# The first FFN matrix of a transformer step as 2x2 blocks in seven products, in six phases

## The chip, the cores and the metric

The kernel runs on one core of one Trainium2 chip. Times are microseconds (us) on the device for one execution. TensorE (PE in the profile, its weight loads PEld) does the matrix products, VectorE (DVE) and ScalarE (ACT) the elementwise work, GpSimd (POOL) masks and small copies, SyncE (SP) issues the DMAs.

## What is computed

One layer of a streaming encoder for 512 prompt rows and 8 x 16 sample rows, 640 rows of 1024 values in all: three token mixers with gates, cross-attention, and a SwiGLU FFN with 2816 hidden channels, each between two RMS norms with a residual. The change concerns the FFN:

```python
def swiglu(h, w_in, w_out):
    g, u = jnp.split(h @ w_in, 2, axis=-1)
    return (jax.nn.silu(g) * u) @ w_out
...
    h = rmsnorm(x, p['norm_ffn_pre'][l])
    x = x + rmsnorm(swiglu(h, p['w_ffn_in'][l], p['w_ffn_out'][l]), p['norm_ffn_post'][l]).astype(x.dtype)
```

All inputs and outputs are 32-bit floats.

## The kernel before

Every large matrix product is made from two parts of each operand: `split` (L141) writes the leading bits of a tile as a cast on ACT and what is left as a subtraction on DVE, and three matmuls (leading x leading, and the two mixed ones) are accumulated for each block of 128 rows of the contraction. Weights arrive by DMA in `raw` tiles (three buffers, L67) and are split into `wh` and `wl` (four buffers each) by `split_w`.

The last stage before the FFN is the output projection of the cross-attention, `ProjD` (L856). Its `finish` (L877) goes over the five tiles of 128 rows: the products of the second column half, the norm, the addition to the residual `X` in SBUF, and the norm ahead of the FFN (`normed`, L187). Two tiles behind, `after_xo` (L1122) transposes the normed rows on TensorE and splits them into `fT_h` and `fT_l` (8 blocks of 128 channels by 640 rows). The calls for the last two tiles are returned as `behind` and come inside the FFN.

The FFN runs in two phases (`ffn_phase`, L1136) of eleven channel units. A unit (`ffn_unit`, L1147) is 128 gate and 128 up channels: 24 matmuls into bank `pg`, Silu on ACT, 24 into `pu`, the product on DVE, and the split into `ga_h`, `ga_l`; once for rows 0 to 383 and once for rows 384 to 639 (`PARTS`). Its weights are two `raw` tiles, each from two DMAs of 256 KB. Then the second matrix follows for the eleven channel tiles, in two column halves (L1177): five accumulators of 128 rows by 512 columns, 3 matmuls for each channel tile and accumulator (L1199 to L1201). `finish` (L1208) evicts an accumulator: in phase 0 by a copy on ACT into `Y`, in phase 1 by an addition to `Y` on DVE, the gain, and a sum of squares on ACT. In the last column half each tile of rows is then normed, added to `X` and stored.

The framework puts the instructions of each engine into one fixed order, by the order of the program and by when their operands are ready in its own model, and adds the waits. Each engine takes its instructions in that order. A tile with n buffers makes a new writer wait for the readers of the n-th last one. PSUM has eight banks, two for each of the tags `g`, `t`, `z` and `o`. Silu and the pair Ln and Exp (`rstd_of`, L146) need different tables on ACT, and a change of table is a load.

## Time and profile before

| | |
|---|---|
| median of three runs | 1338.93 us (1330.9, 1338.93, 1339.3) |
| the profiled execution: its time | not listed by itself among the three; 1330.9 is below its span |
| the profiled execution: its span, first to last instruction | 1332.9 us |
| instructions | 21503 |
| mean granted TensorE clock | 0.995 of full speed |
| DMA | 128.65 MB, 97 GB/s over the span |

The profile is of one execution. A busy time counts an engine's instructions. A matmul row lasts from the start of its weights' use to the modelled end of its last column, so neighbouring rows overlap: the pace is the distance of their starts. In the chain of waits one row is a stretch of instructions on one engine, each followed back to what released it.

### The profile page before, as it was taken

The page shows a single profiled execution, that of the slowest core. Times are in us where ns is not written, and L with a number is a line of the kernel's source. Part 1 is how long each engine was busy: PE and PEld are TensorE (multiplying, and loading weights), DVE is VectorE, ACT ScalarE, POOL GpSimd, SP SyncE. Part 2 cuts the span into 40 slices and gives each one's busy share as a digit, 9 for nine tenths or more (in the row PEclk, how much of TensorE's full clock was granted, in tenths as well). Part 3 has the DMA queues.
Part 4 walks back from the last instruction along what each step waited for, and adds up shares of the span by engine and source line. Part 5 has one row for each costly group of instructions (what it writes and reads, how often), then busy time and mean ns, then how long its engine had stood idle before and what let it go on. Part 6 is the DMA issues. An engine that isn't in the chain of part 4 may idle for free.

```text
span 1332.9 us, 21503 instructions
## 1 busy us (share of the span) xinstructions
PE 1313.9 (99%) x8754; PEld 1194.7 (90%) x8754; DVE 629.3 (47%) x1242; ACT 541.5 (41%) x1087; POOL 41.3 (3%) x162
## 2 busy tenths in 40 slices
PE   9999999999999999999999999999999999999997
PEld 8998678988999999979988878899999889999986
DVE  6434775485587454547444434742322112322235
ACT  5324665454353454435444523642222222322222
POOL 2001111001000000000000000000000000000000
PEclk9999999999999999999999999999999999999999
DMA  7324231202412222422368821232222223232212
GB/s 233 112 77 128 82 97 49 60 1 66 116 30 68 84 88 75 144 94 95 127 227 296 270 79 33 70 105 64 84 75 72 72 73 86 64 95 64 75 52 79
DMA packets 134296, 128.65 MB, mean 97 GB/s; under 512 B 15670, under 2 KB 116613, under 8 KB 134197
## 3 DMA queue, kind: packets, MB, share of 16 engines
q1 hardware_dynamic: 133909, 126.98, 30.7%
q8 instruction: 69, 1.13, 0.3%
q0 software_dynamic: 288, 0.29, 0.1%
q14 instruction: 30, 0.25, 0.1%
HBM read 119.10 MB, written 8.15 MB: 95 GB/s over the span
## 4 chain that ended last, share of the span: by engine, by line
PE 93%; DVE 3%; DMA 2%; ACT 1%; issue 0%; SPq 0%; POOL 0%; DVEq 0%; ACTq 0%
PE ps_g L114 12%; PE pu L114 12%; PE pg L114 12%; PE ps_d L114 8%; PE ps_n L114 7%; PE ps_xq L114 4%; PE ps_b L114 4%; PE acc L1201 4%; PE acc L1199 4%; PE acc L1200 4%; PE ps_qk L114 3%; PE pl L718 2%; PE ps_xk L114 2%; PE ps_xv L114 1%; PE z L505 1%; PE xo L1074 1%
## 5 line engine op out<-in xcount | busy, mean ns | idle before, releaser
L1157 DVE TENSOR_TENSOR s<-pu,s 128x384 f32<-128x384 f32 (+1 forms) x44 | 21.5, 488 | 125.2 <-PE pu L114 125.2
L1199 PE MATMUL acc<-wh_o,ga_h 128*128 128x512 f32 (+1 forms) x168 | 64.5, 384 | 0.0
L1201 PE MATMUL acc<-wh_o,ga_l 128*128 128x512 f32 (+1 forms) x168 | 64.4, 384 | 0.0
L1200 PE MATMUL acc<-wl_o,ga_h 128*128 128x512 f32 (+1 forms) x168 | 64.3, 382 | 0.0
L89 DVE TENSOR_TENSOR wl_o<-raw_o,wh_o 128x1024 fp32r<-128x1024 f32 (+1 forms) x24 | 27.2, 1135 | 77.7 <-ACT wh_o L83 77.5
L1154 ACT ACTIVATE s<-pg 128x384 f32<-128x384 f32 (+1 forms) x44 | 19.3, 439 | 89.6 <-PE pg L114 89.6
L813 ACT ACTIVATE sgm<-ps_g 128x320 f32<-128x320 f32 x48 | 21.0, 437 | 66.0 <-PE ps_g L114 65.9
L83 ACT CAST wh_o<-raw_o 128x1024 fp32r<-128x1024 f32 (+1 forms) x24 | 23.5, 978 | 49.8 <-PE acc L1201 36.7
L143 ACT CAST ga_h<-s 128x384 fp32r<-128x384 f32 (+1 forms) x32 | 14.7, 459 | 63.2 <-DVE s L1157 63.2
L1201 PEld LDWEIGHTS acc<-wh_o,ga_l 128*128 128x128 f32 x168 | 31.5, 188 | 6.8
L1200 PEld LDWEIGHTS acc<-wl_o,ga_h 128*128 128x128 f32 x168 | 31.6, 188 | 6.7
L1199 PEld LDWEIGHTS acc<-wh_o,ga_h 128*128 128x128 f32 x168 | 31.5, 188 | 6.5
L718 PEld LDWEIGHTS pl<-X 96*120 96x120 f32 (+6 forms) x256 | 28.9, 181 | 6.4 <-issue 3.7
L814 DVE TENSOR_SCALAR sgm<-sgm 128x320 f32<-128x320 f32 x48 | 15.5, 325 | 40.4 <-ACT sgm L813 40.3
L718 PE MATMUL pl<-X 96*120 96x64 f32 (+6 forms) x256 | 30.5, 263 | 2.8 <-DVE X L714 2.7
L114 PE MATMUL ps_d<-wh_xo,oT_h 128*128 128x512 f32 x80 | 32.4, 405 | 0.0
L114 PE MATMUL ps_d<-wh_mix,mT_h 128*128 128x512 f32 x80 | 31.9, 398 | 0.0
L114 PE MATMUL ps_d<-wl_xo,oT_h 128*128 128x512 f32 x80 | 31.7, 396 | 0.0
L114 PE MATMUL ps_d<-wh_xo,oT_l 128*128 128x512 f32 x80 | 31.6, 396 | 0.0
L114 PE MATMUL ps_d<-wl_mix,mT_h 128*128 128x512 f32 x80 | 31.6, 395 | 0.0
L114 PE MATMUL ps_d<-wh_mix,mT_l 128*128 128x512 f32 x80 | 31.4, 392 | 0.0
L815 ACT ACTIVATE sgm<-sgm 128x320 f32<-128x320 f32 x48 | 22.5, 469 | 15.8 <-DVE sgm L814 15.7
(1207 smaller groups left out, 4442.1 us busy)
## 6 DMA issues: line engine op xcount, KB each, us to landing
raw_o<-in_w_ffn_out_dram SPq DMA_DIRECT2D x20, 512.0 KB, 3.8
kc<-in_cache_mem_k_dram SPq DMA_DIRECT2D x16, 512.0 KB, 4.8
vc<-in_cache_mem_v_dram SPq DMA_DIRECT2D x16, 512.0 KB, 5.4
raw_mix<-in_w_mix_out_dram SPq DMA_DIRECT2D x8, 512.0 KB, 4.2
raw_xo<-in_w_xo_dram SPq DMA_DIRECT2D x8, 512.0 KB, 6.2
kn<-in_cache_sb_k_dram SPq DMA_DIRECT2D x24, 128.0 KB, 2.5
vn<-in_cache_sb_v_dram SPq DMA_DIRECT2D x24, 128.0 KB, 2.7
out_dram<-X SPq DMA_DIRECT2D x10, 256.0 KB, 2.0
```

The source lines that it names most:

```text
L83: nc.scalar.copy(wh, raw)
L89: (eng or nc.vector).tensor_tensor(wl, raw, wh.bitcast(F32), ALU.subtract)
L114: ins = nc.tensor.matmul(ps, a, b, start=(j == 0), stop=(j == len(todo) - 1))
L718: nc.tensor.matmul(pl[0:nk, h], X[:, h, 0:nk], mv_, start=True, stop=True)
L813: nc.scalar.activation(s, ps, AF.Exp, scale=-1.0)
L814: nc.vector.tensor_scalar(s, s, 2.0 ** 63, None, ALU.min)
L815: nc.scalar.activation(s, s, AF.Ln, bias=1.0)
L1154: nc.scalar.activation(s, pg, AF.Silu)
L1157: nc.vector.tensor_tensor(s, pu, s, ALU.mult)
L1199: nc.tensor.matmul(ps, ah, wh[:, kk, lo:hi], start=(first and kk == 0), stop=False)
L1200: nc.tensor.matmul(ps, ah, wl[:, kk, lo:hi], start=False, stop=False)
L1201: nc.tensor.matmul(ps, al, wh[:, kk, lo:hi], start=False, stop=(last and kk == nk - 1))
```

## The change

Let the 1024 input channels be two halves, the 640 rows two halves of 320, and the gate and up channels of a unit the two column halves. The product of these 2x2 blocks is made from seven block products P1 to P7 (Winograd's form of Strassen's method) in place of eight, for 20 of the 22 units. Each is 4 blocks of 128 channels x 3 matmuls of 320 columns. The right-hand sides are sums of weight blocks (`sums`, four operations on DVE for each unit), the left-hand sides sums of row blocks (`s_prep`, once, on the transposed rows that `after_xo` also copies into `X`), and each is split into two parts. The products share banks: some accumulate onto a bank after ACT or DVE has read it.

The columns of `fT` are put in another order (`cols`): a half of the sample rows and two prompt tiles make 320. The two first units stay plain, with the Silu behind the last Exp and four different banks, and run beside the last two tiles of rows. Six phases of 4, 3, 3, 4, 4 and 4 units follow each other, each with its part of the second matrix; the order of TensorE is written out by hand there (`manual_schedule`). Every phase adds its accumulators to `Y`, which now lies in the memory of `X`; the residual is written to DRAM (`xd`) and read back in the last phase. There all of a tile's columns are finished before the next tile. A weight tile of the second matrix holds one channel tile and all 1024 columns, before two channel tiles and 512 columns. `ProjD.finish` takes the tiles in the order 4, 0, 1, 2, 3, puts the sum into its `Y` and the normed rows into `X`. The rest of the diff takes comments out.

New lines, and context, without the lines that are taken out (those of `ffn_phase`, printed above):

```diff
-        def finish(self, wpool, gain2, done):
+        def finish(self, wpool, gain2, done, order=tuple(range(NT)), in_y=False):
             self.ws = load_w512(self.w2d, 512, 512, self.name + "1")
+            res = self.Y if in_y else X
...
+                    nc.vector.scalar_tensor_tensor(res[:, i, cs], self.Y[:, i, cs], r, X[:, i, cs], ALU.mult, ALU.add)
+                xns[i] = normed(wpool, res[:, i, :], gain2, 3, X[:, i, :] if in_y else None)
...
+    xd = tc.dram_tile([NT, P, D], F32, name="xd")
...
     def after_xo(i, xn):
+        for b, tp in enumerate(transposed(xn)):
+            ks = slice(4 * b, 4 * b + 4)
+            nc.scalar.copy(x32(i)[:, ks, :], tp)
+            src = tp.rearrange("p k (two c) -> p k two c", two=2) if i == 4 else tp
+            split(cols(fT_h[:, ks], i), cols(fT_l[:, ks], i), src)
+    behind = xo.finish(None, g2, after_xo, (4, 0, 1, 2, 3), True)
+    for i in (4, 0, 1, 2, 3):
+        nc.sync.dma_start(xd[i], Y[:, i, :])
...
+    Y = X
+    fw = open_pool("fw", "right")
+    g_post = gain_tile(fw, norm_ffn_post, "gpost")
+    ga_h = fw.tile([P, 4, TOK], F32R, name="ga_h")
+    ga_l = fw.tile([P, 4, TOK], F32R, name="ga_l")
...
+    S_h = hpool.tile([P, 16, H2], F32R, tag="th", name="S_h")
+    S_l = hpool.tile([P, 16, H2], F32R, tag="tl", name="S_l")
+    sub, addop = ALU.subtract, ALU.add
+    def s_prep(a, b, o):
+        w = a.shape[-1]
+        nc.vector.tensor_tensor(b[:, 4:8], b[:, 0:4], b[:, 4:8], addop)
+        nc.vector.tensor_tensor(b[:, 0:4], a[:, 0:4], b[:, 0:4], sub)
+        nc.vector.tensor_tensor(a[:, 0:4], b[:, 4:8], a[:, 0:4], sub)
+        nc.vector.tensor_tensor(a[:, 4:8], a[:, 4:8], a[:, 0:4], sub)
+        split(S_h[:, 0:8, o:o + w], S_l[:, 0:8, o:o + w], b)
+        split(S_h[:, 8:16, o:o + w], S_l[:, 8:16, o:o + w], a)
...
+    def g_split(k, s):
+        (ph_, sh_), (pl_, sl_) = gt(k)
+        two = lambda t: t.rearrange("p (t c) -> p t c", t=2)
+        split(two(ph_), two(pl_), s[:, :, 64:H2])
+        split(two(sh_), two(sl_), s[:, :, 0:64])
...
+    AH = {"P1": ((fT_h, fT_l), 0, 0), "P2": ((fT_h, fT_l), 4, 0), "P4": ((fT_h, fT_l), 4, H2),
+          "P7": ((S_h, S_l), 0, 0), "P5": ((S_h, S_l), 4, 0), "P6": ((S_h, S_l), 8, 0), "P3": ((S_h, S_l), 12, 0)}
...
+        def load(self):
+            wv = w1.rearrange("(k p) c -> p k c", p=P)
+            c0 = self.n * P
+            self.ra = ring.tile([P, 2, 4, P], F32, tag="raw", bufs=3, name="ra")
+            self.rb = ring.tile([P, 2, 4, P], F32, tag="raw", bufs=3, name="rb")
+            for j in range(2):
+                nc.sync.dma_start(self.ra[:, j], wv[:, 0:4, c0 + j * FF:c0 + j * FF + P])
+            for j in range(2):
+                nc.sync.dma_start(self.rb[:, j], wv[:, 4:8, c0 + (1 - j) * FF:c0 + (1 - j) * FF + P])
+        def sums(self):
+            self.ta = fpool.tile([P, 2, 4, P], F32, tag="ta", bufs=1, name="ta")
+            self.t4 = fpool.tile([P, 1, 4, P], F32, tag="t4", bufs=1, name="t4")
+            ra, rb, ta = self.ra, self.rb, self.ta
+            nc.vector.tensor_tensor(ta[:, 1], rb[:, 0], ra[:, 1], sub)
+            nc.vector.tensor_tensor(ta[:, 0], ra[:, 1], ra[:, 0], sub)
+            nc.vector.tensor_tensor(ra[:, 1], ta[:, 1], ra[:, 0], addop)
+            nc.vector.tensor_tensor(self.t4[:, 0], rb[:, 1], ra[:, 1], sub)
+        def parts(self, which):
+            src, names = {"ra": (self.ra, ("P1", "P6")), "ta": (self.ta, ("P5", "P7")),
+                          "rb": (self.rb, ("P3", "P2")), "t4": (self.t4, ("P4",))}[which]
+            pool, tags, bufs = (fpool, ("t4h", "t4l"), 1) if which == "t4" else (ring, ("wh", "wl"), 4)
+            h = pool.tile(list(src.shape), F32R, tag=tags[0], bufs=bufs, name="wh_f")
+            l = pool.tile(list(src.shape), F32R, tag=tags[1], bufs=bufs, name="wl_f")
+            split(h, l, src)
+            for j, nm in enumerate(names):
+                self.w[nm] = (h[:, j], l[:, j])
+        def mm(self, nm, ps, start, stop=True):
+            (ah, al), k0, c0 = AH[nm]
+            bh, bl = self.w[nm]
+            todo = []
+            for kk in range(4):
+                a, b = ah[:, k0 + kk, c0:c0 + H2], al[:, k0 + kk, c0:c0 + H2]
+                todo += [(bh[:, kk], a), (bh[:, kk], b), (bl[:, kk], a)]
+            for j, (w_, m_) in enumerate(todo):
+                nc.tensor.matmul(ps, w_, m_, start=(start and j == 0), stop=(stop and j == 11), skip_group_check=True)
+        def p1(self):
+            self.X = bank([P, H2], "g", "fX")
+            self.mm("P1", self.X, True)
+            self.p1s = fpool.tile([P, H2], F32, tag="p1s", bufs=1, name="p1s")
+            nc.scalar.copy(self.p1s, self.X)
...
+        def p2(self):
+            self.Yb = bank([P, H2], "t", "fY")
+            self.mm("P2", self.Yb, True)
+            self.s = fpool.tile([P, 2, H2], F32, tag="s", bufs=1, name="s")
+            self.c = fpool.tile([P, 2, H2], F32, tag="c", bufs=1, name="c")
+            nc.vector.tensor_tensor(self.s[:, 0], self.Yb, self.p1s, addop)
+            nc.scalar.activation(self.s[:, 0], self.s[:, 0], AF.Silu)
...
+        def p3(self):
+            self.mm("P3", self.Zb, False)
+            nc.vector.tensor_tensor(self.c[:, 0], self.Zb, self.u2, addop)
+        def p4(self):
+            self.mm("P4", self.X, False)
+            nc.scalar.activation(self.s[:, 1], self.X, AF.Silu)
+            nc.vector.tensor_tensor(self.s, self.s, self.c, ALU.mult)
+            g_split(self.k, self.s)
...
+    def plain_units(mids):
+        ws = [load_w8(w1, [(k * P, P), (FF + k * P, P)], f"f{k}") for k in range(2)]
+        st = [fpool.tile([P, 2, H2], F32, tag="sc"[k], bufs=1, name="s") for k in range(2)]
+        for part, (t0, w) in enumerate(PARTS):
+            sl = slice(t0, t0 + w)
             for k in range(2):
+                s = st[k].rearrange("p t c -> p (t c)")
+                pg = bank([P, w], "gz"[k], "pg")
+                gemm_T(pg, ws[k], 0, fT_h, fT_l, t0, w, 1)
+                with tc.issue_after(xo.exp.ins):
+                    nc.scalar.activation(s[:, sl], pg, AF.Silu)
+                pu = bank([P, w], "go"[k], "pu")
+                gemm_T(pu, ws[k], P, fT_h, fT_l, t0, w, 1)
+                nc.vector.tensor_tensor(s[:, sl], pu, s[:, sl], ALU.mult)
+                if part == 0:
+                    mids[k]()
+                else:
+                    g_split(k, st[k])
...
+    def out_mms(i, k, wp, c0, w, ps, first, last):
+        wh, wl = wp[0], wp[1]
+        gh, gl = gt(k)
+        ah, al = rows_of(gh, i), rows_of(gl, i)
+        nc.tensor.matmul(ps, ah, wh[:, 0, c0:c0 + w], start=first, stop=False)
+        nc.tensor.matmul(ps, ah, wl[:, 0, c0:c0 + w], start=False, stop=False)
+        nc.tensor.matmul(ps, al, wh[:, 0, c0:c0 + w], start=False, stop=last)
...
+    PHASES = (4, 3, 3, 4, 4, 4)
...
+    s_mid = [lambda: (behind[0](), s_prep(x32(4)[:, :, 0:64], x32(4)[:, :, 64:128], 0)),
+             lambda: (behind[1](), s_prep(x32(0), x32(2), 64), s_prep(x32(1), x32(3), 192))]
+    for ph, nk in enumerate(PHASES):
+        us = units[ph]
+        if ph == 0:
+            plain_units(s_mid)
+            us = us[2:]
+            us[0].load()
+            us[0].sums()
+            for w_ in ("ra", "ta", "rb", "t4"):
+                us[0].parts(w_)
+        with tc.manual_schedule(engines={mybir.EngineType.PE}):
+            for j, u in enumerate(us):
+                nx_ = us[j + 1] if j + 1 < len(us) else None
+                if nx_:
+                    nx_.load()
+                if j == 0:
+                    u.p1()
+                    u.p5()
+                    if nx_:
+                        nx_.sums()
+                        nx_.parts("ra")
+                    u.p2()
+                    u.p6()
+                    if nx_:
+                        nx_.parts("ta")
+                        nx_.p1()
+                    u.p7()
+                    if nx_:
+                        nx_.parts("rb")
+                    u.p3()
+                    u.p4()
+                    if nx_:
+                        nx_.parts("t4")
+                    continue
+                u.p6()
+                if nx_:
+                    nx_.sums()
+                    nx_.parts("ra")
+                u.p5()
+                if nx_:
+                    nx_.parts("ta")
+                u.p2()
+                u.p7()
+                if nx_:
+                    nx_.parts("rb")
+                    nx_.p1()
+                u.p3()
+                if nx_:
+                    nx_.parts("t4")
+                u.p4()
...
+        wo = [w2_parts(w2_load(n0 + k)) for k in range(nk)]
+        nxt = units[ph + 1][0] if not last_ph else None
+        if last_ph:
+            Xr = hpool.tile([P, NT, D], F32, tag="th", name="Xr")
+            for i in range(NT):
+                nc.sync.dma_start(Xr[:, i, :], xd[i])
+        else:
+            nxt.load()
...
+            if ph == 0:
+                nc.scalar.copy(dst, ps)
+                return
...
+            if not last_ph:
+                nc.vector.tensor_tensor(dst, ps, dst, addop)
+                return
...
+            acc = [(0, 512, bank([P, 512], "zzoog"[i], "acc")) for i in range(NT)]
+            early = nk - 2
+            for k in range(early):
                 for i in range(NT):
+                    out_mms(i, k, wo[k], 0, 512, acc[i][2], k == 0, False)
+            if not last_ph:
+                for i in range(NT):
+                    for k in range(early, nk):
+                        out_mms(i, k, wo[k], 0, 512, acc[i][2], False, k == nk - 1)
+                    finish(i, acc[i], 0)
+                acc = [(512, 512, bank([P, 512], "zzoog"[i], "acc")) for i in range(NT)]
+                for k in range(nk):
+                    for i in range(NT):
+                        out_mms(i, k, wo[k], 512, 512, acc[i][2], k == 0, k == nk - 1)
+                        if k == nk - 1:
+                            finish(i, acc[i], 1)
+                nxt.sums()
+                for w_ in ("ra", "ta", "rb", "t4"):
+                    nxt.parts(w_)
+                continue
+            order = (0, 1, 2, 3, 4)
+            for q, i in enumerate(order):
+                for k in range(early, nk):
+                    out_mms(i, k, wo[k], 0, 512, acc[i][2], False, k == nk - 1)
+                finish(i, acc[i], 0)
+                if q == NT - 1:
+                    ps2 = [(512 + 256 * n, 256, bank([P, 256], "tt"[n], "acc")) for n in range(2)]
+                else:
+                    ps2 = [(512, 512, bank([P, 512], "ttgt"[q], "acc"))]
+                for n, part in enumerate(ps2):
+                    for k in range(nk):
+                        out_mms(i, k, wo[k], part[0], part[1], part[2], k == 0, k == nk - 1)
+                    finish(i, part, 1 + n)
                 ss = stat.tile([P, 1], F32, tag="ss", name="ss")
+                nc.vector.tensor_reduce(ss, ssp[:, i, 0:1 + len(ps2)], AX.X, ALU.add)
                 r = rstd_of(ss, 1, D)
...
+                    nc.vector.scalar_tensor_tensor(Xr[:, i, cs], Y[:, i, cs], r, Xr[:, i, cs], ALU.mult, ALU.add)
+                    nc.sync.dma_start(yo[:, cs], Xr[:, i, cs])
```

## Rows read from the trace of the kernel before

**Rows 1.** The page, part 1: busy time, share of the span, instructions of each engine.
```profile
PE 1313.9 (99%) x8754; PEld 1194.7 (90%) x8754; DVE 629.3 (47%) x1242; ACT 541.5 (41%) x1087; POOL 41.3 (3%) x162
```

**Rows 2.** The page, part 4: the chain that ended last, by engine.
```profile
PE 93%; DVE 3%; DMA 2%; ACT 1%; issue 0%; SPq 0%; POOL 0%; DVEq 0%; ACTq 0%
```

**Rows 3.** Windows of the FFN: start:end length, busy by engine, clock, DMA share, GB/s.
```profile
860.56:891.17 30.61, 30.33 (x209) 29.77 (x209) 17.85 (x35) 17.82 (x35) 0.00 (x0) 1.00 0.34 100
891.17:1017.87 126.70, 126.70 (x866) 126.70 (x865) 37.83 (x55) 35.59 (x56) 0.00 (x0) 1.00 0.27 79
1017.87:1094.48 76.61, 76.61 (x331) 61.94 (x331) 13.50 (x14) 16.84 (x22) 0.00 (x0) 1.00 0.20 62
1094.48:1249.84 155.36, 155.36 (x1061) 155.24 (x1060) 46.35 (x66) 44.13 (x68) 0.00 (x0) 1.00 0.28 82
1249.84:1325.88 76.04, 76.03 (x360) 62.77 (x359) 32.03 (x56) 18.35 (x39) 0.00 (x0) 1.00 0.18 66
```

**Rows 4.** All waits of TensorE from 830 to 900 us: total, times, longest.
```profile
PE tp L179 <- DVE s L1157: 0.3, 1, 0.3
```

**Rows 5.** Chain in order of time, one unit's groups: start, length, engine, tile, count.
```profile
1126.85 4.19 PE pu L114 x24
1131.04 2.81 PE pg L114 x24
```

**Rows 6.** The same chain in the mixer's gates, first and last of ten periods.
```profile
502.57 3.50 PE ps_g L114 x24
...
551.10 3.53 PE ps_g L114 x24
```

**Rows 7.** Groups of DVE from 700 us on: shapes, count, busy us, mean ns, idle before.
```profile
L89 DVE TENSOR_TENSOR wl_o<-raw_o,wh_o 128x1024 fp32r<-128x1024 f32 x20 | 24.5, 1223 | 56.3 <-ACT wh_o L83 56.1
L89 DVE TENSOR_TENSOR wl_o<-raw_o,wh_o 128x512 fp32r<-128x512 f32 x4 | 2.8, 693 | 21.4 <-ACT wh_o L83 21.4
L144 DVE TENSOR_TENSOR oT_l<-tp_so,oT_h 128x128 fp32r<-128x128 f32 x8 | 2.3, 290 | 3.4 <-ACT oT_h L143 3.4
L1157 DVE TENSOR_TENSOR s<-pu,s 128x384 f32<-128x384 f32 x22 | 12.3, 558 | 118.4 <-PE pu L114 118.4
L1157 DVE TENSOR_TENSOR s<-pu,s 128x256 f32<-128x256 f32 x22 | 9.2, 419 | 6.8 <-PE pu L114 6.8
```

**Rows 8.** Groups of ACT from 700 us on, the same columns.
```profile
L83 ACT CAST wh_o<-raw_o 128x1024 fp32r<-128x1024 f32 x20 | 21.0, 1049 | 26.0 <-PE acc L1201 12.9 <-PE pu L114 4.9 <-DMA raw_o<-in_w_ffn_out_dram 4.1
L1154 ACT ACTIVATE s<-pg 128x384 f32<-128x384 f32 x22 | 10.8, 492 | 52.2 <-PE pg L114 52.2
L1154 ACT ACTIVATE s<-pg 128x256 f32<-128x256 f32 x22 | 8.5, 385 | 37.4 <-PE pg L114 37.4
L143 ACT CAST fT_h<-tp 128x512 fp32r<-128x512 f32 x10 | 5.7, 584 | 5.6 <-PE tp L179 5.5
L143 ACT CAST oT_h<-tp_so 128x128 fp32r<-128x128 f32 x8 | 2.1, 266 | 5.3 <-PE tp_so L1022 5.3
L1154 ACT ACT_TABLE_LOAD x2 | 2.6, 1283 | 0.0
```

**Rows 9.** DMA issues: tile, queue, count, KB each, median us from issue to landing.
```profile
raw_o<-in_w_ffn_out_dram SPq DMA_DIRECT2D x20, 512.0 KB, 3.8
...
raw_f_5a<-in_w_ffn_in_dram SPq DMA_DIRECT2D x4, 256.0 KB, 4.2
```

**Rows 10.** DVE in order of time: the last tile's low parts in the stretch of 860.56.
```profile
880.59 0.69 DVE L144 TENSOR_TENSOR fT_l<-tp,fT_h 128x512 fp32r<-128x512 f32 x1
```

**Rows 11.** DVE in order of time in the last pass, one tile of rows.
```profile
1311.24 0.69 DVE L1217 TENSOR_TENSOR y<-acc,Y 128x512 f32<-128x512 f32 x1 [0.71 <-PE acc L1201]
...
1312.73 0.16 DVE L1230 TENSOR_REDUCE ss<-sspf 128x1 f32<-128x2 f32 x1
...
1316.11 0.69 DVE L1217 TENSOR_TENSOR y<-acc,Y 128x512 f32<-128x512 f32 x1 [0.77 <-PE acc L1201]
```

**Rows 12.** The end of the chain: the issue of the last output.
```profile
1328.92 0.66 DVEq L1281
```

More of the change, by code (lines that the diff above doesn't have):

```diff
@@ L144, in split @@
         nc.vector.tensor_tensor(l, src, h.bitcast(F32), ALU.subtract)
+    last_exp = [None]
     def rstd_of(ss, n, width):
@@ L875, in start @@
             self.unit(i, 0)
-        def finish(self, wpool, gain2, done):
+        def finish(self, wpool, gain2, done, order=tuple(range(NT)), in_y=False):
             self.ws = load_w512(self.w2d, 512, 512, self.name + "1")
-            xns = []
-            for i in range(NT):
-                self.unit(i, 1, (lambda: done(i - 2, xns[i - 2])) if i > 1 else None)
+            res = self.Y if in_y else X
+            xns = {}
+            for j, i in enumerate(order):
+                self.unit(i, 1, (lambda: done(order[j - 2], xns[order[j - 2]])) if j > 1 else None)
                 ss = stat.tile([P, 1], F32, tag="ss", name="ss")
@@ new lines, in tile_hybrid_stream_step, with finish @@
+    PHASES = (4, 3, 3, 4, 4, 4)
+    ssp = stat.tile([P, NT, 3], F32, tag="sspf", bufs=1, name="sspf")
+    units, n = [], 0
+    for ph, nk in enumerate(PHASES):
+        units.append([Unit(n + k, k) for k in range(nk)])
+        n += nk
+    flat = [u for ph in units for u in ph]
+    Xr = None
+    s_mid = [lambda: (behind[0](), s_prep(x32(4)[:, :, 0:64], x32(4)[:, :, 64:128], 0)),
+             lambda: (behind[1](), s_prep(x32(0), x32(2), 64), s_prep(x32(1), x32(3), 192))]
+    for ph, nk in enumerate(PHASES):
+        us = units[ph]
[46 more added lines that the diff above has]
+                u.p4()
+        last_ph = ph == len(PHASES) - 1
+        if last_ph:
+            tc.keep_in_program_order(nc.scalar.preload_act_table_set("natural_log_exp_and_others"))
+        n0 = units[ph][0].n
+        wo = [w2_parts(w2_load(n0 + k)) for k in range(nk)]
+        nxt = units[ph + 1][0] if not last_ph else None
+        if last_ph:
+            Xr = hpool.tile([P, NT, D], F32, tag="th", name="Xr")
[3 more added lines that the diff above has]
+            nxt.load()
+        def finish(i, part, n):
+            c0, w, ps = part
+            cs = slice(c0, c0 + w)
+            dst = Y[:, i, cs]
+            if ph == 0:
[4 more added lines that the diff above has]
+                return
+            y = fw.tile([P, 512], F32, tag="y", bufs=2, name="y")[:, 0:w]
+            nc.vector.tensor_tensor(y, ps, dst, addop)
+            nc.vector.tensor_tensor(dst, y, g_post[:, cs], ALU.mult)
+            junk = fw.tile([P, 512], F32, tag="junk", bufs=1, name="junk")
+            nc.scalar.activation(junk[:, 0:w], y, AF.Square, accum_out=ssp[:, i, n:n + 1])
+        with tc.manual_schedule(engines={mybir.EngineType.PE}):
+            acc = [(0, 512, bank([P, 512], "zzoog"[i], "acc")) for i in range(NT)]
+            early = nk - 2
+            for k in range(early):
+                for i in range(NT):
+                    out_mms(i, k, wo[k], 0, 512, acc[i][2], k == 0, False)
[27 more added lines that the diff above has]
+                    finish(i, part, 1 + n)
```

142 lines of the change are left out of this document (39 added, 103 removed).

## Prediction

> **What bounds the kernel now.** I first read the page for the engines and the chain of waits. TensorE is busy for 1313.9 of 1332.9 us, VectorE (DVE) for 47%, ScalarE (ACT) for 41% [rows 1], and the chain that ended last is 93% TensorE [rows 2]. Then I cut the FFN into windows [rows 3]: two stretches of nothing but first-matrix units (9 and 11 of them), the stretch before them with two units beside the last norms, and the two stretches of the second matrix. In all of them TensorE is busy from end to end at a granted clock of 1.00, while DVE is busy for 30% and ACT for 28% of the unit stretches (84.2 and 79.7 us of 282.1). TensorE waits for another engine once in that region, for 0.3 us [rows 4]. So here a column that TensorE does not stream is time, and work on DVE and ACT is free until it is late.
>
> **What is removed: columns.** The 9 + 11 = 20 units in the two stretches [rows 3] take 126.70 + 155.36 = 282.06 us, 14.10 us each; one unit is four groups of 24 matmuls, 4.2 + 4.2 us on 384 columns and 2.8 + 2.8 us on 256 [rows 5]. That is 96 matmuls, 30,720 columns. A seven-product unit has 7 x 12 = 84 matmuls of 320 columns, 26,880 columns. The pace at 320 columns is in this trace, in the gates of the mixer: ten periods of 24 + 9 matmuls from 502.57 to 551.10 us [rows 6], 48.53 us for 330, or 0.1471 us each. So a new unit takes 84 x 0.1471 = 12.35 us, 20 of them 247.1 us, and **35.0 us** go. The other two units keep their 384 + 256 split and their price. The second matrix keeps its 2 x 22 x 5 x 3 = 660 matmuls of 512 columns, so its 76.61 us for half of them stand (0.232 us each).
>
> The Trainium skill ("TensorE: Matmul & The Clock Gate", Back-to-back issue gap) prices a warm matmul at N/2.4 ns plus some 2.5 ns: 109, 136 and 162 ns for 256, 320 and 384 columns. The trace has 118, 147 and 175 [rows 5, 6], about 8% more at each, so the measurement decides; by the page the saving would be 32.6 us, an estimate.
>
> **What is added on DVE and ACT for each unit.** DVE subtractions and additions between two tiles of SBUF cost 1.22 us for 1024 elements a partition, 0.69 for 512, 0.56 for 384, 0.42 for 256 and 0.29 for 128 [rows 7]. A unit does four sums of 512 (2.8 us), the low parts of three tiles of 1024 and one of 512 (4.4), three additions out of PSUM of 320 (not in the trace; between 0.42 and 0.56 each, I take 0.49: 1.5), one product of 640 (between 0.69 and 1.22, I take 0.83), and the low parts of the result, 512 and 128 (1.0). Together 10.4 us of DVE in 12.35 us of TensorE, 84%, where before it was 84.2/20 = 4.2. ACT does three casts of 1.05 and one of 0.59, three copies and two Silu of 320 (between 0.39 and 0.49, 0.44 each: 2.2), and casts of 512 and 128 (0.85): 6.8 us, 55% [rows 8]. Both fit, so I cost them at nothing inside a unit, with the products as cover. If that cover fails, rival A prices it. What each product waits for has this slack: the accumulation onto a bank must wait until ACT or DVE has read it, and the written order puts one or two other products (1.76 us each) between; one 1.22 us instruction in front plus 0.49 of its own is 1.7 us, so in places with one product between (the first and the last unit of a phase) the cover is just used up. I put 0.3 us per phase there.
>
> **Weights.** A unit still brings four transfers of 256 KB. The load of the next unit's second half needs the buffer of the current unit's first half (three raw buffers), so there is a loop from one unit to the next: landing 4.2 [rows 9], sums 2.8, cast 1.05, low part 1.22: 9.3 us, plus what DVE does in between. It is under 12.35 us, and every phase starts with both halves loaded, so over three or four units it does not catch up. Cost 0.
>
> **Phases.** Six instead of two. At each change the second matrix starts on channel tiles that are long done: the last two are held back, so the last unit's Silu, product, cast and low part (0.44 + 0.83 + 0.59 + 0.69 = 2.6 us in sequence) stand beside 15 or 30 matmuls of 0.232 us, 3.5 or 7.0 us. The weights of the second matrix, one tile of 1024 per channel tile as now, are split during the last unit, and the next first unit is prepared during the second matrix; the 40 added evictions into Y (0.69 us of DVE each [rows 7]) come one per 0.70 us at worst. From all of this 0 to 1.5 us per change; with the term above I take **+3 us** for the phases (0 to 8).
>
> **The start.** Before the first seven-product unit, its seven left-hand operands must exist, and they need the last tile of rows. In the stretch from 860.56 to 891.17 DVE is busy for 17.85 of 30.61 us, and the last tile's low parts end at 881.3 [rows 3, 10]. Added there: for the samples four steps of 256 and two low parts of 512 (4 x 0.42 + 2 x 0.69 = 3.1), for the prompt twice four steps of 512 and two of 1024 (10.4), and the four weight sums (2.8): 16.3 us, so 34.2 in the 32.4 us until the second product begins (P1 needs none of the sums of rows). DVE is thus full, with the second half of the work behind the last tile. That TensorE runs dry here is the one clear new wait. At least 1.8 us; if all that comes after 881.3 (both prompt halves 10.4, two weight splits 2.4, products and low parts of the plain units 3, with about 4 us of casts not overlapped) ran alone, it would end at 901, 8 us late. I take **+5 us** (1 to 10), with the first seven-product unit's own weights in it. Silu is put behind the last Exp, which takes away the change of tables between Silu and Ln or Exp, 1.28 us of ACT for each load [rows 8]; that helps ACT carry ten added copies of 0.59. These copies lie beside the output projection of the cross-attention: **+0.5 us** (0 to 2).
>
> **The residual in DRAM.** 2.5 MB go out, 2.5 MB come back. Both are off the chain: the write has until the first result tile is stored, the read is issued when the last unit ends and is first needed some 11 us later, each 512 KB landing in 3.8 us [rows 9]. Cost 0, bounds 0 and 3 us.
>
> **The tail.** Now a tile of rows has 21 matmuls (4.87 us) in the last pass, and DVE is idle for 0.77 us of it [rows 11]. In the new last phase both column halves of a tile are finished one after the other: 18 matmuls, 4.19 us, against DVE work of 4.10 (4.87 less 0.77) plus a second eviction with its gain, 1.49 us (1311.24 to 1312.73): 5.6 us. DVE falls behind by 1.4 us a tile, over four tiles 5.6, less what moves into its waits for Ln and Exp. I take **+3.5 us** (1 to 6) after the last matmul, where 3.0 us of chain stand now between the last matmul at 1325.9 and the issue of the last output at 1328.9 [rows 3, 12].
>
> **Sum.** -35.0 + 3 + 5 + 0.5 + 3.5 = -23 us. The profiled execution has a span of 1332.9 us; of the three times (1330.9, 1338.93 and 1339.3) the lowest is below that span, so I take it as the median, 1338.9, with 6.0 us around the span. 1338.9 - 23 = **1316 us**.
>
> **Rivals.** *A, the queues of DVE and ACT bind inside the units.* For it: 84% load in a fixed order, where every low part waits for a cast (the idle time before wl_o is put down to ACT [rows 7]); if 3.7 us of DVE's other 6.4 in a unit come to lie inside the weight loop above, that loop takes 13.0 us. Against it: the phases are short. Price: 0.65 us on the 14 units that follow another seven-product unit, 9 us: 1325. The Trainium skill ("TensorE: Matmul & The Clock Gate", specification table) says that the queues of ScalarE and VectorE are strictly first in, first out; no row here shows an overtaking. *B, slower than before.* The same hand-overs run in series in every unit: DVE waits for each of its casts and evictions, so a unit takes 10.4 + 6.8 = 17.2 us. Then 20 x (17.2 - 14.1) + 12 = +74 us, 1413. It decides once a unit takes over 13.5 us (14.1 less the 12 us of other terms over 20). Against it: today casts of the next unit run under low parts of the last, and 10.4 us lie under 12.35. *C, everything is hidden.* The start costs 1 us, the tail 1.5, the rest 0.5: -32 us, 1307. Against it: DVE is full in the start. *D, the change does not do what it says*, because the pace at 320 columns is worse in products of 12 that change banks: at 0.155 us a unit takes 13.0, the saving is 22 us, 1329. Against it: the gates' nine-matmul products keep the same pace [rows 6].
>
> **How the numbers follow.** Forecast (1308 to 1324) 0.70; C 0.10; A or D 0.15; B 0.05. About 1% is what a measurement of this kernel can tell from no change (the three times span 0.6%): 1325.5 us. The forecast, C and a third of A and D lie below it: faster 0.85. Same 0.10, the other two thirds. Slower 0.05. The range goes from 1304, below C by the spread of the times, to 1330, the far end of A and D.
>
> **What would show it.** In the profile after: products of 12 matmuls in 1.76 us and units 12.4 us apart; DVE at 80% there with TensorE still at 99% or more; a wait of TensorE of some microseconds for a DVE or ACT part of the S tiles near 893 us, and little else; DVE without idle time over the last 25 us. Wrong would be units of 13 us or more, waits of TensorE for weight parts in every unit, or a granted clock below 1.00 in the units.

## The result and the profile after

After: 1300.67 us median of four runs (1298.68 to 1303.65). Before, timed beside it: 1337.56 us, four runs (1330.9 to 1339.3). The ratio is 0.9738, 95% interval 0.9709 to 0.9767: faster, by more than forecast, and below the range. Timed again beside the experiments, before had medians of 1333.49, 1332.79 and 1334.59 us (9 to 13 runs each). After was not timed again, but with its 1300.67 us these give a gain of 32.1 to 33.9 us, so about 33 us is the better size. The profiled execution of after took 1298.68 us, with a span of 1297.0.

The page of after, parts 1 and 4, which answer to [rows 1, 2]:

```profile
PE 1275.6 (98%) x8493; PEld 1156.5 (89%) x8493; DVE 776.2 (60%) x1458; ACT 596.5 (46%) x1198; POOL 41.2 (3%) x162
...
PE 91%; DVE 4%; ACT 2%; DMA 2%; issue 1%; SPq 0%; POOL 0%; DVEq 0%; ACTq 0%
```

TensorE lost 38.3 us of busy time and DVE gained 147 us; the chain is still mostly TensorE (91%, before 93%). The windows of the FFN of after, columns as in [rows 3]: the plain stretch, then unit stretches and second matrices in turn, and the last second matrix with the tail:

```profile
857.68:888.58 30.90, 30.18 (x210) 29.86 (x210) 30.52 (x55) 21.17 (x44) 0.00 (x0) 1.00 0.37 119
888.58:913.20 24.62, 24.62 (x169) 24.61 (x169) 16.91 (x24) 13.42 (x21) 0.00 (x0) 1.00 0.39 128
913.20:940.99 27.79, 27.79 (x123) 22.52 (x122) 12.43 (x17) 10.11 (x16) 0.00 (x0) 1.00 0.20 57
940.99:977.95 36.96, 36.96 (x253) 36.96 (x253) 24.14 (x34) 19.09 (x31) 0.00 (x0) 1.00 0.33 100
977.95:998.80 20.85, 20.85 (x92) 16.90 (x92) 12.86 (x19) 3.88 (x6) 0.00 (x0) 1.00 0.17 51
...
1056.61:1105.86 49.25, 49.25 (x338) 49.25 (x337) 35.31 (x50) 24.88 (x41) 0.00 (x0) 1.00 0.32 97
...
1259.92:1297.00 37.08, 27.89 (x133) 22.91 (x131) 24.29 (x56) 12.24 (x36) 0.00 (x0) 0.93 0.36 135
```

Read the third column, TensorE, against the second, the length. They are equal in every stretch from 888.58 on but the last, whose 9.19 us without TensorE are the tail. 24.62, 36.96 and 49.25 us are two, three and four units of 12.31 us. All waits of TensorE from 840 us to the end, which answer to [rows 4], and two pieces of the chain inside one unit:

```profile
PE pg L114 <- ACT fT_h L143: 0.7, 1, 0.7
```

```profile
1061.89 5.28 PE fX L1237 x36
1067.17 1.75 PE fZ L1237 x12
```

That is one wait in 457 us, and products of 12 matmuls in 1.75 to 1.76 us. The account of the two executions, in us, before to after:

| stretch | before | after | |
|---|---|---|---|
| all that comes ahead of `xo.finish` | 823.93 | 820.91 | -3.0, not the change |
| `xo.finish` | 36.63 | 36.77 | +0.1 |
| two plain units | 30.61 | 30.90 | +0.3 |
| 20 units | 282.06 | 246.27 | -35.8 |
| second matrix (TensorE) | 152.64 | 152.96 | +0.3 |
| tail, behind the last matmul | 7.0 | 9.2 | +2.2 |

The change's own part is -32.9 us, inside the 32.1 to 33.9 of the medians. The 3.0 us come from stages that both kernels share. In before's execution the granted clock there was 0.91 from 400 to 420 us and 0.92 from 770 to 790, in after's 1.00 in both stretches: 20 x 0.09 + 20 x 0.08 = 3.4 us, an estimate. Executions of kernels that are alike up to the FFN differ there by as much, as those below show.

### The profile page after: what moved, and what is told of

Read it like the earlier page. It is cut to its first block, busy times and chain, and to the rows that moved or that the text cites. A ratio compares the mean times of both kernels' runs of the same rounds, so it can differ in the third digit from the quotient of the medians.

```text
span 1297.0 us, 21377 instructions
## 1 busy us (share of the span) xinstructions
PE 1275.6 (98%) x8493; PEld 1156.5 (89%) x8493; DVE 776.2 (60%) x1458; ACT 596.5 (46%) x1198; POOL 41.2 (3%) x162
## 3 DMA queue, kind: packets, MB, share of 16 engines
q1 hardware_dynamic: 132501, 132.23, 32.4%
## 4 chain that ended last, share of the span: by engine, by line
PE 91%; DVE 4%; ACT 2%; DMA 2%; issue 1%; SPq 0%; POOL 0%; DVEq 0%; ACTq 0%
PE ps_g L114 13%; PE fX L1237 11%; PE ps_d L114 8%; PE ps_n L114 8%; PE fZ L1237 5%; PE ps_xq L114 4%; PE ps_b L114 4%; PE acc L1308 4%; PE acc L1309 4%; PE acc L1310 3%; PE ps_qk L114 3%; PE fY L1237 3%; PE pl L721 2%; PE ps_xk L114 2%; PE ps_xv L114 1%; PE z L508 1%
## 5 line engine op out<-in xcount | busy, mean ns | idle before, releaser
L1237 PE MATMUL fX<-fT_h,wl_f 128*128 128x320 f32 x160 | 49.5, 309 | 0.0
L1237 PE MATMUL fX<-fT_l,wh_f 128*128 128x320 f32 x160 | 49.4, 309 | 0.0
L1237 PE MATMUL fZ<-S_h,wl_f 128*128 128x320 f32 x160 | 49.4, 309 | 0.0
L1237 PE MATMUL fX<-fT_h,wh_f 128*128 128x320 f32 x160 | 49.4, 309 | 0.0
L1237 PE MATMUL fX<-S_h,wh_f 128*128 128x320 f32 x160 | 49.4, 309 | 0.0
L1237 PE MATMUL fX<-S_l,wh_f 128*128 128x320 f32 x160 | 49.4, 309 | 0.0
L1237 PE MATMUL fZ<-S_l,wh_f 128*128 128x320 f32 x160 | 49.4, 309 | 0.0
L1237 PE MATMUL fZ<-S_h,wh_f 128*128 128x320 f32 x160 | 49.4, 309 | 0.0
L1237 PE MATMUL fX<-S_h,wl_f 128*128 128x320 f32 x160 | 49.3, 308 | 0.0
L1393 DVE TENSOR_TENSOR X<-acc,X 128x512 f32<-128x512 f32 x40 | 27.2, 690 | 17.9 <-PE acc L1310 17.9
```

What stands on the lines that cost most here:

```text
L1237: nc.tensor.matmul(ps, w_, m_, start=(start and j == 0), stop=(stop and j == 11), skip_group_check=True)
L1393: nc.vector.tensor_tensor(dst, ps, dst, addop)
```

## The experiments

All kernels are after with one edit. As executions differ by several us ahead of the FFN, each is cut by four landmarks that the trace gives: the first `pg` matmul, the first `fX`, the first `acc` and the start of the last `acc` matmul. The last column counts from the start of the last `acc` matmul. e3, e4, e5, e8, e9 and e10 were timed once each, so they are read from their landmarks and waits, and not from their times. Lengths between landmarks in us:

| | `pg` starts | to `fX` | to `acc` | to last `acc` | to the end |
|---|---|---|---|---|---|
| after | 857.5 | 30.9 | 24.6 | 374.5 | 9.5 |
| e1, eight products | 857.7 | 30.9 | 28.1 | 406.0 | 9.2 |
| e3, four more sums | 861.7 | 30.9 | 32.0 | 374.5 | 9.2 |
| e4, eight more sums | 861.0 | 35.2 | 34.1 | 415.6 | 9.2 |
| e5, start loaded | 864.4 | 30.9 | 28.8 | 374.5 | 9.4 |
| e6, gain on GpSimd | 862.4 | 30.9 | 24.6 | 375.2 | 10.0 |
| e8, ten phases | 863.4 | 30.9 | 24.6 | 406.3 | 11.4 |
| e9, Silu not held | 859.0 | 30.9 | 25.2 | 374.5 | 9.2 |
| e10, no gain | 860.5 | 30.9 | 24.6 | 374.5 | 8.4 |
| e11, last phase's order | 859.3 | 30.9 | 24.6 | 374.5 | 8.5 |

Before has 465.2 us from the first `pg` to the last `acc` and 7.3 from there to the end.

**e1: the seventh product bought back.**

```diff
             self.mm("P1", self.X, True)
+            self.mm("P1", self.X, True)
```

> Product P1 is run twice in each of the 20 units (the second run starts the bank anew), so every unit has eight products of 12 matmuls again. Theory: TensorE binds in the units, so the time is that of the changed kernel plus 20 x 1.755 = 35 us, about 1336 us, ratio to before 0.998 to 1.003, and units 14.07 us apart. Rival: DVE or the weight loads already hold the units near 12.3 us, so part of the eighth product is hidden: +25 us or less, 1326 us.

Measured: 1336.82 us (10 runs), ratio 1.0027, interval 1.0006 to 1.0048. The two unit columns grow by 3.5 and 31.5 us, 35.0 for 20 products or 1.75 each, and no wait appears. With eight products, and so with before's number of columns, the whole gain is gone: it lies in the columns of TensorE. The theory's time came, the rival's did not.

**e2: the arrangement without the seven products.** All 22 units plain, with the sums of rows and of weights left out.

```diff
-            for j, u in enumerate(us):
...
+        for u in units[ph][2 if ph == 0 else 0:]:
+            plain_unit(u.n, u.k)
```

> Only the seven products are undone: all 22 units plain (384 + 256 columns, 96 matmuls), the row sums left out as nobody reads them; the six phases, the residual in DRAM, the column order and the last phase stay. Theory: the gain is in the columns alone, and the rest of the change costs some 2 to 3 us, nearly all at the tail: 1339 to 1340 us, ratio to before 1.002. Rival: the part of the measured gain that the FFN stretches of the two profiles don't show (36.9 us between the medians against 33 us there) belongs to the new structure: 1333 us, ratio 0.997.

Measured: 1341.3 us, ratio 1.0056, interval 1.0039 to 1.0073. From the first `pg` to the last `acc` it takes 465.9 us, before 465.2: phases, order and residual in DRAM, taken together, gain nothing there and cost 0.7 us at most. What is slower is the tail, 15.2 us against 7.3, which puts the time above both expectations. In that kernel ACT changes its table twice for every norm of the last phase:

```profile
1309.81 1.28 ACT L153 ACT_TABLE_LOAD   x1
1311.10 0.30 ACT L153 ACTIVATE y<-ss,eps_t 128x1 f32<-128x1 f32 x1
1311.42 1.28 ACT L154 ACT_TABLE_LOAD   x1
```

Ten such loads stand in its last phase, four of them (5.1 us) behind the start of the last `acc` matmul; after has two loads in the whole FFN and none in the tail. So the longer tail is this edit's and no cost of the change; why the framework placed the loads so was not followed up.

**e3 and e4: more DVE work in every unit.** The first sum of weights is done five times in e3 (shown) and nine times in e4.

```diff
-            nc.vector.tensor_tensor(ta[:, 1], rb[:, 0], ra[:, 1], sub)
+            for _ in range(5):
+                nc.vector.tensor_tensor(ta[:, 1], rb[:, 0], ra[:, 1], sub)
```

> The first of the four weight sums of a unit is done five times: four more DVE instructions of 512 elements in each of the 20 units, results unchanged. Theory (an instruction occupies DVE for the distance to the next start, 0.60 us, not for its row's 0.69; a unit leaves DVE some 3.5 us): +2.4 us per unit are covered, and only the first units, where DVE is full, are late: +1 to +5 us in all. Rival (the prices of the prediction, 10.4 us and 0.69 each): 13.2 us per unit, +18 us. Second rival (the sums stand ahead of what the next product waits for): every unit is late by up to 2.4 us, +30 us or more.

> The same sum done nine times: eight more DVE instructions of 512 elements in each unit. Theory: +4.8 us per unit on 8.8 us is 13.6 us against 12.31 us of TensorE, so units that follow each other are DVE-bound, by 1.3 us on some 14 units, and the start by some 5: +15 to +30 us. Rival (prices of the prediction): 15.9 us per unit, +72 us.

Measured: e3 1310.05 us, e4 1356.81. e3 is above all that my theory allowed (+1 to +5 us), and the table shows where: the first phase takes 7.4 us more, all the rest nothing (374.5, to the tenth); the stretch ahead of the first `pg`, which the edit does not touch, gives 4.2. The waits of TensorE in the FFN of e3, and its windows around them (columns as in [rows 3]):

```profile
PE fX L1238 <- ACT wh_f L143: 2.9, 1, 2.9
PE fX L1238 <- DVE wl_f L144: 1.1, 2, 0.7
```

```profile
875.00:900.00 25.00, 23.56 (x174) 23.03 (x174) 24.71 (x38) 13.98 (x24) 0.00 (x0) 1.00 0.13 44
900.00:925.00 25.00, 21.75 (x128) 21.03 (x127) 14.94 (x20) 11.40 (x18) 0.00 (x0) 0.86 0.28 86
...
1075.00:1100.00 25.00, 25.00 (x173) 24.98 (x172) 23.49 (x36) 13.46 (x23) 0.00 (x0) 1.00 0.28 85
```

4.0 us of waits, and behind them a granted clock of 0.86 over 25 us, worth 25 x 0.14 = 3.5: together that is the 7.4. So 18 units carry four more sums for nothing, with DVE at 94% of a stretch, and the first two do not: the start has no room. In e4 the rest does not hold either: 54.9 us more between the landmarks, above the theory's 15 to 30 and below the rival's 72. Its waits of TensorE, a window with the one behind it, and from 930 us on a wait of DVE and one of its rows:

```profile
PE fX L1238 <- ACT wh_f L143: 25.9, 14, 4.2
PE fX L1238 <- DVE wl_f L144: 9.4, 14, 0.7
```

```profile
1175.00:1200.00 25.00, 20.09 (x130) 18.78 (x129) 22.08 (x33) 10.85 (x17) 0.00 (x0) 1.00 0.15 43
1200.00:1225.00 25.00, 22.78 (x144) 22.25 (x143) 20.35 (x29) 11.06 (x20) 0.00 (x0) 0.93 0.36 106
```

```profile
DVE ta L1215 <- DMA rb<-in_w_ffn_in_dram: 13.1, 12, 3.0
...
1281.72 2.14 DVE L1215 TENSOR_TENSOR ta<-rb,ra 128x512 f32<-128x512 f32 x3
```

DVE's 35.31 us over four units of after are 8.8 a unit. An instruction of 512 takes 0.60 us from start to start (shown below), but 0.72 where the same sum follows itself: three in 2.14 us. So e3 has 11.2 to 11.7 us a unit and e4 13.6 to 14.6, on either side of the 12.31 that TensorE needs. In e3 nothing waits behind the start. In e4, behind the first phase, TensorE waits for 26.4 us in 12 places, and a clock of 0.93 in five stretches of 25 us makes 8.8: 35.2 of the 41.1 us that the table shows there; some 6 are not accounted for. The chain ahead of such a wait runs along DVE, but DVE is not full everywhere: it is busy for 22.08 of the 25 us shown and waits itself, 12 times and 13.1 us in all, for the transfer of `rb`, which needs a `raw` buffer. So the loop over the weight buffers, rival A's, may take part in e4; these runs do not separate it from DVE's load. The prices of the prediction would have put e3 at 10.4 + 2.8 = 13.2 us, over the edge, and that did not happen. The unit's own DVE work thus has at least 2.4 us in hand.

**e5: more DVE work in the start alone.** Four more low parts of 1024.

```diff
-             lambda: (behind[1](), s_prep(x32(0), x32(2), 64), s_prep(x32(1), x32(3), 192))]
+             lambda: (behind[1](), s_prep(x32(0), x32(2), 64), extra(), s_prep(x32(1), x32(3), 192))]
...
+    def extra():
+        for _ in range(4):
+            nc.vector.tensor_tensor(S_l[:, 0:8, 64:192], x32(2), S_h[:, 0:8, 64:192].bitcast(F32), sub)
```

> Four more low parts of 1024 (1.22 us each by their rows, 1.14 from start to start) stand on DVE in the stretch before the first seven-product unit. Theory (that stretch has no slack: DVE is busy for 30.5 of its 30.9 us and the parts land just in time): TensorE waits about 4 to 5 us at the first products of that unit, and the time is 1304 to 1307, with a lower granted clock in the 25 us behind the wait. Rival (the start has several us in hand, since the S tiles are ready some us ahead of their products): no new wait of TensorE there, 1299 to 1303. By the prediction's own way of adding (+5 already there, which was not): 1305 or more in any case.

Measured: 1309.74 us. In the table the first phase is 4.2 us longer and all else as in after; the other 6.9 us lie ahead of the first `pg`, in stages that the edit does not touch (the clock was 0.83 in 400 to 420 us and 0.91 in 740 to 760 of that execution), so the time alone would have misled. The new waits and the window after them:

```profile
PE fX L1237 <- DVE wl_f L144: 1.9, 2, 1.4
PE fZ L1237 <- DVE wl_f L144: 1.5, 1, 1.5
```

```profile
900.00:925.00 25.00, 23.87 (x158) 23.44 (x159) 17.65 (x24) 12.13 (x19) 0.00 (x0) 1.00 0.35 109
```

The waits sum to 3.4 us. Of 4 x 1.13 = 4.5 us put in, 4.2 come out: the start has less than half a us in hand. It is full, and just not late. The lower clock that I expected behind the waits did not come.

**e6: part of the tail's DVE work on GpSimd.**

```diff
-            nc.vector.tensor_tensor(dst, y, g_post[:, cs], ALU.mult)
+            nc.gpsimd.tensor_tensor(dst, y, g_post[:, cs], ALU.mult)
```

> The multiplication by the gain at the evictions of the last phase goes from DVE to GpSimd, which is idle there. Theory (the 9.2 us between the last matmul and the end are DVE falling behind tile by tile): DVE's work per tile of rows drops by about 1.2 us, and the end comes 1 to 3 us earlier: 1298 to 1300, ratio about 0.972. Rival (the tail is the latency of one tile's sequence, matmul, eviction, sum of squares, norm, output, not DVE's load): GpSimd is slower for the same tile, the sequence gets longer, and the time is 1301 to 1304, ratio 0.975 or more.

Measured: 1302.31 us (5 runs), ratio 0.9773, interval 0.9758 to 0.9789, and in the table 0.7 us more ahead of the last `acc` and 0.5 behind it. The rival's numbers came; whether its reason holds, e10 and e11 ask. One tile on GpSimd and the DVE instruction beside it:

```profile
1281.92 2.55 POOL L1397 TENSOR_TENSOR X<-y,gpost 128x512 f32<-128x512 f32 x2 [2.45 <-DVE y L1396]
```

```profile
1283.81 0.68 DVE L157 SCALAR_TENSOR_TENSOR t<-y,m 128x1 f32<-128x1 f32 x1 [0.83 <-ACT y L154]
```

The multiplication takes 1.28 us for each 512 columns where DVE takes 0.69. And the DVE instruction of one element, 0.22 us in after, takes 0.68 and ends at 1284.49, with the GpSimd pair (1284.47); the next two tiles have the same, 0.67 and 0.74 us. The Trainium skill ("SBUF — State Buffer", Who interferes with whom) says that a DVE instruction with two SBUF inputs contends with a GpSimd instruction that reads SBUF, and that such contention is an exclusive lock. By that, this row is the wait for the pair's end, and the trace agrees: it ends 0.02 us behind it.

**e8: ten phases.**

```diff
-    PHASES = (4, 3, 3, 4, 4, 4)
+    PHASES = (4, 2, 2, 2, 2, 2, 2, 2, 2, 2)
...
-                        out_mms(i, k, wo[k], 0, 512, acc[i][2], False, k == nk - 1)
+                        out_mms(i, k, wo[k], 0, 512, acc[i][2], k == 0, k == nk - 1)
...
```

> Phases of 4 and nine times 2 units in place of 4, 3, 3, 4, 4, 4: ten phases in place of six, with no channel tile of the phase held long before the second matrix starts. Theory (a phase costs nothing as long as the second matrix has tiles that were done long ago): with two tiles a phase, the last unit's Silu, product, cast and low part are only partly covered, and each of the nine short phases shows a wait of TensorE of 1 to 3 us: +9 to +27, 1310 to 1328, the clock lower behind each wait. Rival (a phase is free however short it is): no new waits, 1299 to 1304. By the price of the prediction (0.5 us a phase): +2, 1303.

Measured: 1338.26 us; 31.8 us more between the first and the last `acc`, 3.5 for each short phase, above the theory's 9 to 27. The waits:

```profile
PE acc L1308 <- ACT ga_h L143: 16.9, 9, 2.2
PE acc L1310 <- DVE ga_l L144: 3.0, 7, 0.4
PE acc L1308 <- DVE y L1396: 1.3, 1, 1.3
```

Nine waits for the last unit's cast, 1.9 us each, one per short phase. With 0.6 us for `c` the waits sum to 21.8 us, and a clock of 0.93 in three stretches of 25 us makes 5.3; some 5 us are not accounted for, and the tail grew by 2 us as well. So in these runs a phase is free while its second matrix can start on channel tiles that are long done. With one or two of three or four tiles in hand it is free, with none it costs what the prediction had called 2.6 us of sequence, and more.

**e9: the Silu not held behind the last Exp.**

```diff
-                with tc.issue_after(xo.exp.ins):
-                    nc.scalar.activation(s[:, sl], pg, AF.Silu)
+                nc.scalar.activation(s[:, sl], pg, AF.Silu)
```

> Silu of the two plain units is no longer held behind the last Exp, so ACT changes its table between Silu and Ln or Exp while it also copies the residual. Theory (the start is bound by DVE, ACT has room): some loads of 1.28 us come back on ACT, TensorE waits under 2 us more, 1299 to 1303. Rival (ACT is on the path there too, through the sums of squares and the norm that release DVE's work on the last rows): three to six loads land on it, +4 to +8 us, 1305 to 1309.

Measured: 1300.64 us; five table loads in the FFN in place of two, one new wait of 0.3 us for `wl_f`, the first phase 0.6 us longer. In this one run that part of the change is worth about half a us, and ACT is not on the path of the start: the theory's time came.

**e10 and e11: the tail, by load and by order.** e10 leaves out the multiplication by the gain in the last phase. e11 keeps all instructions and only lets TensorE take them so that DVE can start earlier.

```diff
-            y = fw.tile([P, 512], F32, tag="y", bufs=2, name="y")[:, 0:w]
-            nc.vector.tensor_tensor(y, ps, dst, addop)
-            nc.vector.tensor_tensor(dst, y, g_post[:, cs], ALU.mult)
+            nc.vector.tensor_tensor(dst, ps, dst, addop)
+            y = dst
```

```diff
-                for i in range(NT):
+                for i in range(2 if last_ph else NT):
                     out_mms(i, k, wo[k], 0, 512, acc[i][2], k == 0, False)
...
+                for k in range(early):
+                    if q + 2 < NT:
+                        out_mms(q + 2, k, wo[k], 0, 512, acc[q + 2][2], k == 0, False)
```

> The last phase leaves out the multiplication by the gain of the FFN's output norm (11 DVE instructions, about 7 us in all); everything else stands. Theory (DVE's load in the last 25 us sets the end: 5.0 us of DVE against 4.2 us of TensorE for each tile of rows): the stretch from the last matmul to the end goes from about 9.2 us to 7 or less. Rival (the sequence of the last tile alone sets it): only the one or two multiplications in that sequence go, and the stretch stays at 8.5 or more. The stretch is read from the trace, since the time of one execution moves by several us elsewhere.

> Last phase, same instructions in another order on TensorE: the early channel tiles are multiplied for the first two tiles of rows only, and for each later tile behind the tile two before it, so that the first eviction comes 4.2 us earlier and TensorE takes 5.6 us for each tile after that in place of 4.2. Theory (DVE falls behind tile by tile): DVE then keeps up, the stretch from the last matmul to the end goes from 9.2 to about 7.3 us, and the time to 1298 to 1300, ratio about 0.972; a wait of up to 1 us for the last unit's product can come at the start of the phase, which would take half of it back. Rival (the last tile's own sequence sets the end): 9 us or more as now, 1300 to 1302, ratio 0.974 to 0.976.

Measured: from the last `acc` to the end 8.4 us in e10 (1300.59 us) and 8.5 in e11 (1299.97 us, 5 runs, ratio 0.9741, interval 0.972 to 0.9762), where after and five other kernels with its tail have 9.2 to 9.5. Both theories miss (7 and 7.3 us), and both rivals as well, by less (8.5 and 9 or more): some 0.7 to 1.1 us of the tail is DVE's lag, and the rest stays without it. DVE at the end of e11 shows what that is:

```profile
1288.28 0.41 DVE L1396 TENSOR_TENSOR y<-acc,X 128x256 f32<-128x256 f32 x1
...
1289.50 1.42 DVE L1443 SCALAR_TENSOR_TENSOR Xr<-X,t,Xr 128x512 f32<-128x512 f32 x2
1290.84 0.42 DVE L1396 TENSOR_TENSOR y<-acc,X 128x256 f32<-128x256 f32 x1
```

The last matmul is over at 1289.6, but the eviction of its accumulator, the third row, stands behind the residual of the tile before (L1443) and starts 1.2 us later; its own norm and residual follow. e11 is the fastest kernel of the study by its median, but its interval covers after's: no difference that these runs can tell.

## Why the prediction was right and where it was wrong

The mechanism and the largest term held. **Columns**: forecast -35.0, measured -35.8; a matmul of 320 columns takes 12.31 / 84 = 0.1466 us in the units, 0.1471 in the gates. e1 gives it back. **What hides inside the units**: costed at nothing, and nothing was seen; four more sums a unit (e3) cost nothing either, eight (e4) do. Rivals A and B, the queues binding, fall with that for this kernel, and D with the pace. B's way of adding DVE and ACT in series (17.2 us) was far off. What A and B feared can be made, though: with eight more sums a unit the kernel is slower than before, and there DVE waits for `rb`, as in A's loop. **Weights** and **residual in DRAM** (0): no wait of TensorE for either; the residual was only tried together with the rest of the arrangement, in e2.

What failed is the terms that were to be paid back, 12 us in the sum, 2.9 measured (the 0.5 for the copies ahead was 0.1). It was case C, to which I gave 0.10.

- **The start, +5, measured +0.3.** The step that failed is the sum of 34.2 us of DVE work in 32.4 us. It added 22 instructions at the length of their rows. Rows of DVE overlap, as the start of after shows:

```profile
880.28 0.69 DVE L1171 TENSOR_TENSOR X<-X 128x512 f32<-128x512 f32 x1
880.88 0.28 DVE L144 TENSOR_TENSOR ga_l<-s,ga_h 128x128 fp32r<-128x128 f32 x1
881.08 0.69 DVE L1172 TENSOR_TENSOR X<-X 128x512 f32<-128x512 f32 x1
881.69 0.68 DVE L144 TENSOR_TENSOR wl_f<-t,wh_f 128x512 fp32r<-128x512 f32 x1
882.29 0.69 DVE L1173 TENSOR_TENSOR X<-X 128x512 f32<-128x512 f32 x1
882.89 1.22 DVE L144 TENSOR_TENSOR S_l<-X,S_h 128x1024 fp32r<-128x1024 f32 x1
884.02 0.42 DVE L1292 TENSOR_TENSOR s<-pu,s 128x256 f32<-128x256 f32 x1
```

  A row of 0.69 us keeps DVE for 0.60, one of 1.22 for 1.13, one of 0.28 for 0.20: 0.08 less each. 22 x 0.08 = 1.8 us, and 34.2 becomes 32.4, the room itself. And the samples' four sums (1.7 us by their rows) are done by 845.5 us, ahead of the stretch that they were counted in. The other error is the order: I let the prompt's sums and the first unit's weights run alone behind the last tile. The trace has the samples' low parts at 864.6 us, the first weight sums at 867.1 and the prompt's first at 869.3, in what was idle time of DVE in before. DVE is busy for 30.52 of the 30.90 us, and the second unit's first low part ends at 895.56 us, just as its product starts. "DVE is full" was right; e5 shows how near to the edge it was.

  The Trainium skill ("Perfetto Trace Analysis", Optimizing Scalar/DVE Operations) gives a DVE instruction on SBUF an access overhead of about 60 ns of engine time and says that its profiled latency is about twice this, since the half that is the write acknowledgement overlaps with the next instruction. The rows above agree in kind, with 0.08 us of overlap.

- **Phases, +3, measured +0.3.** The term was mis-sized: 0.3 us per phase where "the cover is just used up", and up to 1.5 per change, were paid nowhere in six phases. That the cover is the reason, and no property of phases, is what e8 shows.
- **The tail, +3.5, measured +2.2.** DVE is nearly without idle time, as forecast, but for less than 25 us: it is busy for 13.23 of the 13.51 us from 1274.96 to 1288.47, and for 19.85 of the last 25. The residuals of four tiles and the eviction of the last accumulator in after, then that eviction in before:

```profile
1274.96 1.42 DVE L1440 SCALAR_TENSOR_TENSOR Xr<-X,t,Xr 128x512 f32<-128x512 f32 x2
1279.45 1.42 DVE L1440 SCALAR_TENSOR_TENSOR Xr<-X,t,Xr 128x512 f32<-128x512 f32 x2
1284.95 1.41 DVE L1440 SCALAR_TENSOR_TENSOR Xr<-X,t,Xr 128x512 f32<-128x512 f32 x2
1288.47 1.41 DVE L1440 SCALAR_TENSOR_TENSOR Xr<-X,t,Xr 128x512 f32<-128x512 f32 x2
1289.79 0.41 DVE L1396 TENSOR_TENSOR y<-acc,X 128x256 f32<-128x256 f32 x1
...
1325.91 0.42 DVE L1217 TENSOR_TENSOR y<-acc,Y 128x256 f32<-128x256 f32 x1
```

  Three periods in 13.51 us are 4.50 us of DVE a tile, where the prediction had 5.6: it summed one tile's sequence with the small waits in it, and in after the work of the neighbouring tiles fills these. Against TensorE's 4.19 the lag is 0.3 us a tile and not 1.4, 1.2 over four tiles, near the 0.7 to 1.1 of e10 and e11. The rest, by these rows, is the order of the last two tiles' work. Both show in one place: the last matmul is over at 1287.8 us (before 1325.9), and the eviction of its accumulator starts 2.0 us later, behind the residual of the tile before, where in before it starts at once. That is nearly all of the 2.2 us. That another order of DVE would give it back was not tried.
- **The baseline.** I took 6.0 us around the span, from a median and a profile of different executions. After's profiled execution has both: 1298.68 less 1297.0 is 1.7 us. Against 1334.6 us (1332.9 + 1.7), my own -23 would have given 1312 and case C's -32 1303, and the range, 4.3 us lower, would have begun just below the measured time. The terms above would have been as wrong.
- **A reading.** The prices for 384, 256 and 128 elements, taken for operations between two tiles of SBUF, are from rows that read PSUM (`pu`, `tp_so`) [rows 7]. After's rows between SBUF tiles have the same at 256 (0.42 us, L1170) and 128 (0.28), so no error came of it.

So the miss of 15.3 us is 9.1 us of hand-overs that did not come, 0.8 of columns, and about 5 of the baseline: before's later medians are 1332.8 to 1334.6, not 1338.9.

## What to carry to other kernels

In this kernel one engine is busy from end to end: work removed from it counted in full, and work added on DVE cost nothing up to some 11 us in a unit of 12.31. Add such work up from the distances of starts, not from the rows' lengths, before you price a queue as nearly full. A hand-over at a change of phase was free as long as something done long before stood in front of it. For a sum of terms take the span and the time of one and the same execution, and compare experiments by landmarks inside the trace: the time alone moved by up to 7 us ahead of every edit.

## What the runs showed of the hardware

The granted clock fell after some waits of TensorE and gave a second loss: in e3 a wait of 2.9 us is followed by 0.86 in the next 25 us, which is part of that stretch at 1.2 GHz in place of 2.4; in e4 stretches of 0.88 and 0.91 go with two waits of 4.2 us, and five of 0.93 with the twelve later ones (up to 1.7 us, and 0.7 right behind); in e8 three of 0.93 go with nine waits of up to 2.2. In e5, with waits of at most 1.5 us, it stayed at 1.00. So e3 paid nearly twice for what it waited. A DVE instruction of 512 elements takes 0.60 us of the engine for a row of 0.69, but 0.72 where the same sum, into the same tile, follows itself (e4). And moving a DVE multiplication to an idle GpSimd cost 1.28 us where DVE takes 0.69, and held DVE besides: an instruction of 0.22 us took 0.68.
